# w1 and the transposed projections of a two-layer block: three 256-column products per weight tile instead of one of 512 and one of 256

## The chip, the core and the metric

The kernel runs on one core of one Trainium2 chip. The metric is the device time of one execution in microseconds (us); less is better. Three runs of the kernel before took 2183.35, 2184.06 and 2186.3 us, with a median of 2184.06 us.

## What is computed

A block of two layers on 256 tokens of width 2048 in fp32. Layer one is a stick-breaking attention with 16 heads, layer two a sparse attention with compressed, selected and windowed keys; behind each stands an MLP with a hidden width of 8192. Cut to what matters here:

```python
def sqrelu_mlp(h, w1, w2):
    return jnp.square(jax.nn.relu(h @ w1)) @ w2

q, k, v = jnp.split(h @ w_qkv, 3, axis=-1)                                # first attention
q, kc, vc, ks, vs, kw, vw, gl = jnp.split(h @ w_in, offs, axis=-1)        # second attention
...
h = h + attention(rms_norm(h, g))
h = h + sqrelu_mlp(rms_norm(h, mlp_norm_g[layer]), mlp_w1[layer], mlp_w2[layer])
```

The change touches `h @ w1` in both layers, q and k of three of the four head groups of the first attention, and kc and vc of the second.

## The kernel before, in words

Nearly all of the work is products of activations with weights that are read once from memory. To keep fp32 accuracy, each operand is split in two parts of type fp32r: hi, the rounded value, and lo, the rest. A product of x and w is the sum of three: hi by hi, hi by lo and lo by hi (the product of the two lo parts is left out).

Weights come in chunks of 128x1024 values (512 KB), either 2 row blocks of 512 columns (KC = 2, NB = 512) or 4 row blocks of 256 columns. SyncE issues the load (`load`, line 139) into a ring of five buffers; ScalarE copies hi into one of four buffers (line 134), VectorE subtracts lo into one of four (line 136). The two rings have 64 spare values (`PAD`) per buffer, so that a chunk can start at an offset: `NEAR` = 0, `FAR` = 16, `LOW` = 52, `SUM` = 48 values.

The activations of the first factor lie in `xs` as [128, 16 row blocks, 2, 256 tokens]: for each block of 128 rows the 256 columns of xhi and right behind them the 256 of xlo.

Where the result is wanted transposed (features on the partitions, tokens on the columns), a weight tile of 128x128 is the stationary operand and x moves:

- `proj_T2` (line 195), used by `group1` for w1: for two chunks at a time, 16 products of a hi tile with the 512 columns of xhi and xlo together (line 203), then 16 of a lo tile with the 256 columns of xhi (line 210). Each of the four 128-feature parts of a block has a PSUM bank of its own: the left half takes hi by xhi and lo by xhi, the right half hi by xlo.
- `proj_T2h` (line 216), used for q and k of head groups 1 to 3 and for kc and vc: the same on chunks of 4 row blocks by 256 columns (lines 224 and 230), with two banks.
- `chunk_T` (line 178), used for q and k of head group 0 alone, in the first stage, whose order of instructions is written out by hand: for each tile hi by xhi and hi by xlo, 256 columns each, then for all tiles lo by xhi (line 185). All three go into the same half bank; two features' parts share a bank. Its hi and lo lie at `FAR`.

As `proj_T2` leaves two halves to be added, `group1` copies the right half to SBUF on ScalarE (line 449) and adds it to the left on VectorE (line 450), four times for a block of 512 features; then one VectorE pass over 128x1024 takes the maximum with zero and multiplies with the token's norm factor (line 451). Squares, their split (lines 455 to 457) and sums for the Strassen form of a part of w2 (lines 462 to 465) follow. `evac_T2` (line 237) does the same for the projections: two copies (line 241), two additions (line 242) and a product with a row (line 243).

An MLP has four groups of 2048 hidden features; a group is `group1` (four blocks of 512 features, their banks taken in turn from the pools `acc` and `att`, four banks each) and then `group2`, the products with w2 (`chunk_N`, line 152, and `chunk_S`, line 245, with 256-column products at line 280). Work of other stages is put between the products by `pump` (line 106), which the product loops call after every eight or so products. Outside the first stage the compiler's scheduler sets each engine's order.

Of the kernel before, what the change touches and what calls it, by code (L numbers as in the profile page):

```python
# [25 lines left out]
KC = 2  # L26
# [13 lines left out]
def hybrid_kernel(  # L40
# [65 lines left out]
    def pump():  # L106
        if beside:
            b = beside[0]
            b[2] += b[1] / KC
            while b[2] >= 1:  # L110
                b[2] -= 1
                y = next(b[0], b)
                if y is b:
                    beside.remove(b)
                if y:
                    break
# [6 lines left out]

    PAD = 64
    NEAR, FAR, LOW, SUM = 0, 16, 52, 48

    def split(raw, o=(NEAR, NEAR)):  # L130
        n = KC * NB
# [14 lines left out]
    def load_split(*where, o=(NEAR, NEAR)):  # L146
        return split(load(*where), o)

    def bank(pool, tag):
        return pool.tile([P, NB], F32, tag=tag, name=tag)  # L150
# [24 lines left out]
                mm(ahi, lo[:, kk, :], k, t, False, last and kk == KC - 1)  # L175
            pump()

    def chunk_T(ps, src, k0, n0, first, last):

        hi, lo = src if isinstance(src, tuple) else load_split(src, k0, KC, n0, NB, o=(FAR, FAR))  # L180
        tiles = [(kk, m) for kk in range(KC) for m in range(NB // P)]

        def mm(w, x, kk, m, s, e):
            o = ps[m // 2][:, (m % 2) * T:(m % 2 + 1) * T]
            nc.tensor.matmul(o, w[:, kk, m * P:(m + 1) * P], x[:, k0 + kk, :], start=s, stop=e, skip_group_check=True)  # L185

        for kk, m in tiles:
            mm(hi, xhi, kk, m, first and kk == 0 and m % 2 == 0, False)
            mm(hi, xlo, kk, m, False, False)
        pump()  # L190
        for kk, m in tiles:
            mm(lo, xhi, kk, m, False, last and kk == KC - 1)
        pump()

    def proj_T2(ps, src, n0):


        for k0 in range(0, KD, 2 * KC):
            parts = [load_split(src, k0 + i * KC, KC, n0, NB, o=(NEAR, LOW)) for i in range(2)]
            tiles = [(k0 + i * KC + kk, m, *(a[:, kk, m * P:(m + 1) * P] for a in parts[i]))  # L200
                     for i in range(2) for kk in range(KC) for m in range(NB // P)]
            for j, (k, m, hi, lo) in enumerate(tiles):
                nc.tensor.matmul(  # L203
                    ps[m], hi, xs[:, k, :, :].rearrange("p a t -> p (a t)"), start=k == 0, stop=k == KD - 1,
                    skip_group_check=True,
                )
                if j % 8 == 7:
                    pump()
            for j, (k, m, hi, lo) in enumerate(tiles):
                nc.tensor.matmul(  # L210
                    ps[m][:, :T], lo, xhi[:, k, :], start=False, stop=k == KD - 1, skip_group_check=True,
                )
                if j % 8 == 7:
                    pump()

    def proj_T2h(src, n0):

        ps = [bank(acc, "acc") for _ in range(2)]
        KH, W = 2 * KC, NB // 2
        for k0 in range(0, KD, KH):  # L220
            hi, lo = load_split(src, k0, KH, n0, W, o=(NEAR, LOW))
            tiles = [(kk, m) for kk in range(KH) for m in range(2)]
            for kk, m in tiles:
                nc.tensor.matmul(  # L224
                    ps[m], hi[:, kk, m * P:(m + 1) * P], xs[:, k0 + kk, :, :].rearrange("p a t -> p (a t)"),
                    start=k0 + kk == 0, stop=k0 + kk == KD - 1, skip_group_check=True,
                )
            pump()
            for kk, m in tiles:
                nc.tensor.matmul(  # L230
                    ps[m][:, :T], lo[:, kk, m * P:(m + 1) * P], xhi[:, k0 + kk, :],
                    start=False, stop=k0 + kk == KD - 1, skip_group_check=True,
                )
            pump()
        return ps

    def evac_T2(dst, ps, row):

        c = small.tile([P, 2, T], F32, tag="part", name="part", bufs=1)
        for j in range(2):  # L240
            nc.scalar.activation(c[:, j, :], ps[j][:, T:], AF.Copy)
            nc.vector.tensor_tensor(dst[:, j, :], ps[j][:, :T], c[:, j, :], op=OP.add)
        nc.vector.tensor_tensor(dst, dst, row.unsqueeze(1).to_broadcast([P, 2, T]), op=OP.mult)

    def chunk_S(ps, src, k0, n0, first, last, ahi, alo, shi, slo, koff=0):

# [67 lines left out]
    def proj_N(src, n0, pool=acc, tag="acc"):  # L314
        ps = [bank(pool, tag) for _ in range(NT)]
        for k0 in range(0, KD, KC):
            chunk_N(ps, src, k0, n0, k0 == 0, k0 + KC == KD, xhi, xlo)
        return ps

    def proj_T(src, n0):  # L320
        ps = [bank(acc, "acc") for _ in range(2)]
        for k0 in range(0, KD, KC):
            chunk_T(ps, src, k0, n0, k0 == 0, k0 + KC == KD)
        return ps

    def split_evac(hi, lo, src, scale=None):
# [103 lines left out]
    def mlp(l, layer, junk, done, last=None):  # L430
# [9 lines left out]
        def group1(fg, pools):  # L440

            for fb in range(D // NB):
                ps = [bank(*pools[fb % 2]) for _ in range(NB // P)]
                proj_T2(ps, w1, fg * D + fb * NB)
                k, n = fb * (NB // P), NB // P
                a = junk.tile([P, n, T], F32, tag="pre", name="pre", bufs=1)
                for j in range(n):
                    c = junk.tile([P, T], F32, tag="part", name="part")
                    nc.scalar.activation(c, ps[j][:, T:], AF.Copy)
                    nc.vector.tensor_tensor(a[:, j, :], ps[j][:, :T], c, op=OP.add)  # L450
                nc.vector.scalar_tensor_tensor(
                    a, a, 0.0, row.unsqueeze(1).to_broadcast([P, n, T]), op0=OP.max, op1=OP.mult
                )
                s = junk.tile([P, n, T], F32, tag="sq", name="sq", bufs=1)
                nc.scalar.activation(s, a, AF.Square)
                nc.scalar.activation(yhi[:, k:k + n, :], s, AF.Copy)
                nc.vector.tensor_tensor(ylo[:, k:k + n, :], s, yhi[:, k:k + n, :].bitcast(F32), op=OP.subtract)

                sv = s.rearrange("p (j kk) t -> p j kk t", kk=2)
                a1, a2 = [[sv[:, :, kk, t * P:(t + 1) * P] for kk in (1, 0)] for t in range(NT)]  # L460
                q = junk.tile([P, 2, 4, P], F32, tag="sums", name="sums", bufs=1)
                nc.vector.scalar_tensor_tensor(q[:, :, 0, :], a2[0], -1.0, a2[1], op0=OP.mult, op1=OP.subtract)
                nc.vector.tensor_tensor(q[:, :, 2, :], a1[0], a2[0], op=OP.subtract)
                nc.vector.tensor_tensor(q[:, :, 1, :], a2[1], q[:, :, 2, :], op=OP.subtract)
                nc.vector.tensor_tensor(q[:, :, 3, :], a1[1], q[:, :, 1, :], op=OP.subtract)
                split_evac(ss[:, 0, k // 2:k // 2 + 2], ss[:, 1, k // 2:k // 2 + 2], q)
# [44 lines left out]
    with tc.tile_pool(name="sbp", bufs=2) as sp:  # L511
# [171 lines left out]
        for hg in range(NH // HG):  # L683
            qT = sp.tile([P, HG, T], F32, name="qT")
            kT = sp.tile([P, HG, T], F32, name="kT")
            v = sp.tile([P, NT, NB], F32, name="v")
            if hg == 0:
                spawn(first_factors(qT, kT), 1)
            else:
                for b in range(2):  # L690
                    evac_T2(qT[:, 2 * b:2 * b + 2, :], proj_T2h(sb_w_qkv[0], hg * NB + b * T), rows[:, 0, :])
                for b in range(2):
                    evac_T2(kT[:, 2 * b:2 * b + 2, :], proj_T2h(sb_w_qkv[0], D + hg * NB + b * T), rows[:, 1, :])
            psv = proj_N(sb_w_qkv[0], 2 * D + hg * NB, *((att, "att") if hg == 0 else ()))
            for t in range(NT):
                nc.scalar.activation(v[:, t, :], psv[t], AF.Copy, scale=factor[0][:, t:t + 1])

            drain()
            spawn(attention(hg, qT, kT, v), 0.6 if hg < NH // HG - 1 else 1.1)
# [20 lines left out]
    with tc.tile_pool(name="nsa", bufs=2) as ap, ExitStack() as last:  # L720
# [255 lines left out]
        for i in range(2):  # L976
            cT = cp.tile([P, G, T], F32, tag="cT", name="cT", bufs=1)
            for b in range(2):
                ps = proj_T2h(w_in, C0 + i * NB + b * T)
                if rstd is None:  # L980
                    rstd = make_rstd("nsa")
                    pb = bcast_rows(rstd)
                    rb = cp.tile([P, T], F32, name="rb2", bufs=1)
                    nc.scalar.activation(rb, pb[:, :T], AF.Copy)
                evac_T2(cT[:, 2 * b:2 * b + 2, :], ps, rb)
            spawn(compress(i, cT), 1.8)


# [117 lines left out]
```

## Time and profile before

| | us |
|---|---|
| median of three runs | 2184.06 |
| the profiled execution | 2184.25 |
| its span, first to last instruction | 2182.2 |
| TensorE products (PE) busy | 2172.6 |
| TensorE weight loads (PEld) busy | 1880.7 |
| VectorE (DVE) busy | 1524.8 |
| ScalarE (ACT) busy | 1210.8 |
| moved by DMA | 405.97 MB, mean 186 GB/s |

Products are pipelined: the time shown for one reaches to the end of its drain, beside which the next one already runs. What a product costs in a dense stretch is the time from its start to the next one's. Lines of the timeline merge products of one kind in succession: the first number is the start of the first, the second the time to the end of the last.

### The profile page before, as it was taken

The numbers are of one execution on the slowest core, as the hardware profiler recorded it, in microseconds if no ns is written. First come the engines' busy times: TensorE is split into PE (matmuls) and PEld (weight loads), VectorE is DVE, ScalarE is ACT, GpSimd is POOL, SyncE is SP. The second block draws the span as 40 slices with busy tenths as digits, with TensorE's granted clock in tenths as the row PEclk, the third lists the DMA queues.
The fourth block names the chain that finished last, engine by engine and source line by source line (L and its number), as shares of the span: only waits on it lengthen the run. The fifth ranks groups of instructions, "written<-read, shape, count | busy, mean of one in ns | idle before, by whom it ended". The sixth has DMA issues, their size and how long they took to land.

```text
span 2182.2 us, 31326 instructions
## 1 busy us (share of the span) xinstructions
PE 2172.6 (100%) x11922; PEld 1880.7 (86%) x11922; DVE 1524.8 (70%) x2096; ACT 1210.8 (55%) x1697; POOL 42.5 (2%) x75
## 2 busy tenths in 40 slices
PE   9999999999999999999999999999999999999999
PEld 9888888888888888888888888888888888888888
DVE  5656656677677677668777877755777676777685
ACT  5555665555455465456555666655554554654553
POOL 0000000000000000000000011000000000000000
PEclk9999999999999999999999999999999999999999
DMA  7655555565665665665667554456656656656664
GB/s 232 206 172 174 157 182 176 181 186 191 205 191 181 216 190 180 217 192 185 206 181 219 160 145 140 137 165 184 188 181 212 193 174 213 193 180 210 191 198 157
DMA packets 260766, 405.97 MB, mean 186 GB/s; under 512 B 13188, under 2 KB 91912, under 8 KB 260616
## 3 DMA queue, kind: packets, MB, share of 16 engines
q1 hardware_dynamic: 259800, 403.52, 59.6%
q8 instruction: 93, 1.52, 0.3%
q10 hardware_dynamic: 816, 0.46, 0.1%
q14 instruction: 57, 0.47, 0.1%
HBM read 401.83 MB, written 2.10 MB: 185 GB/s over the span
## 4 chain that ended last, share of the span: by engine, by line
PE 99%; DVE 0%; POOL 0%; ACT 0%; issue 0%; DVEq 0%; ACTq 0%; POOLq 0%
PE acc L156 31%; PE att L156 13%; PE acc L203 11%; PE att L203 11%; PE acc L210 5%; PE att L210 5%; PE acc L224 5%; PE att L280 4%; PE acc L280 4%; PE acc L230 3%; PE acc L185 2%; PE att L938 1%; PE att L343 1%; PE att L930 0%; PE att L931 0%; PE att L932 0%
## 5 line engine op out<-in xcount | busy, mean ns | idle before, releaser
L136 DVE TENSOR_TENSOR lo<-raw,hi 128x1024 fp32r<-128x1024 f32 x687 | 830.9, 1220 | 386.4 <-issue 170.0
L134 ACT ACTIVATE hi<-raw 128x1024 fp32r<-128x1024 f32 x687 | 726.5, 1059 | 655.7 <-PE acc L156 182.8
L156 PE MATMUL acc<-hi,yhi 128*128 128x512 f32 x640 | 250.7, 392 | 0.0
L156 PE MATMUL acc<-hi,ylo 128*128 128x512 f32 x640 | 249.2, 390 | 0.0
L203 PE MATMUL acc<-xs,hi 128*128 128x512 f32 x1024 | 243.8, 390 | 0.0
L203 PE MATMUL att<-xs,hi 128*128 128x512 f32 x1024 | 243.2, 390 | 0.0
L203 PEld LDWEIGHTS acc<-xs,hi 128*128 128x128 f32 x1024 | 187.8, 188 | 36.2 <-DVE h L399 0.3
L203 PEld LDWEIGHTS att<-xs,hi 128*128 128x128 f32 x1024 | 188.0, 188 | 35.9
L156 PE MATMUL acc<-hi,xs 128*128 128x512 f32 x704 | 177.1, 392 | 0.0
L156 PE MATMUL acc<-lo,yhi 128*128 128x512 f32 x640 | 172.4, 390 | 0.0
L156 PEld LDWEIGHTS acc<-hi,xs 128*128 128x128 f32 x704 | 130.3, 188 | 26.5
L156 PE MATMUL att<-hi,yhi 128*128 128x512 f32 x380 | 148.2, 390 | 0.0
L156 PE MATMUL att<-hi,ylo 128*128 128x512 f32 x380 | 147.9, 389 | 0.0
L156 PEld LDWEIGHTS acc<-lo,yhi 128*128 128x128 f32 x640 | 119.5, 188 | 24.9 <-issue 0.4
L134 ACT ACTIVATE hi<-ts 128x1024 fp32r<-128x1024 f32 x64 | 67.8, 1059 | 130.9 <-DVE ts L260 92.8
L156 PEld LDWEIGHTS acc<-hi,yhi 128*128 128x128 f32 x640 | 120.2, 188 | 23.3 <-ACT yhi L329 0.2
L156 PEld LDWEIGHTS acc<-hi,ylo 128*128 128x128 f32 x640 | 120.2, 188 | 23.2 <-DVE ylo L330 0.2
L210 PEld LDWEIGHTS att<-xs,lo 128*128 128x128 f32 x1024 | 128.4, 188 | 5.2
L254 DVE TENSOR_TENSOR ts<-raw 128x512 f32<-128x512 f32 x64 | 44.2, 691 | 126.3 <-DMA raw<-in_mlp_w_dram 126.3
L210 PEld LDWEIGHTS acc<-xs,lo 128*128 128x128 f32 x1024 | 128.2, 188 | 4.8
L210 PE MATMUL acc<-xs,lo 128*128 128x256 f32 x1024 | 130.1, 278 | 0.0
L210 PE MATMUL att<-xs,lo 128*128 128x256 f32 x1024 | 129.7, 278 | 0.0
(305 smaller groups left out, 3058.1 us busy)
## 6 DMA issues: line engine op xcount, KB each, us to landing
raw<-in_mlp_w_dram SPq DMA_DIRECT2D x512, 512.0 KB, 4.2
raw<-in_sb_w_qkv_dram SPq DMA_DIRECT2D x95, 512.0 KB, 4.0
raw<-in_nsa_w_in_dram SPq DMA_DIRECT2D x50, 512.0 KB, 3.6
raw<-in_sb_w_out_dram SPq DMA_DIRECT2D x32, 512.0 KB, 3.8
raw<-in_nsa_w_in_dram SPq DMA_DIRECT2D x64, 256.0 KB, 3.3
raw<-in_nsa_w_out_dram SPq DMA_DIRECT2D x32, 512.0 KB, 3.8
w1t<-in_nsa_cmp_w_dram SPq DMA_DIRECT2D x8, 512.0 KB, 4.8
h<-in_x_dram SPq DMA_DIRECT2D x8, 256.0 KB, 4.2
```

Of the source, the lines that this page charges most:

```text
L134: nc.scalar.activation(hi, raw, AF.Copy)
L136: nc.vector.tensor_tensor(lo, raw, hi.bitcast(F32), op=OP.subtract)
L156: mm = lambda a, b, k, t, s, e: nc.tensor.matmul(ps[t], a[:, k, t * P:(t + 1) * P], b, start=s, stop=e)
L185: nc.tensor.matmul(o, w[:, kk, m * P:(m + 1) * P], x[:, k0 + kk, :], start=s, stop=e, skip_group_check=True)
L203: nc.tensor.matmul(ps[m], hi, xs[:, k, :, :].rearrange("p a t -> p (a t)"), start=k == 0, stop=k == KD - 1, skip_group_check=True,)
L210: nc.tensor.matmul(ps[m][:, :T], lo, xhi[:, k, :], start=False, stop=k == KD - 1, skip_group_check=True,)
L224: nc.tensor.matmul(ps[m], hi[:, kk, m * P:(m + 1) * P], xs[:, k0 + kk, :, :].rearrange("p a t -> p (a t)"), start=k0 + kk == 0, stop=k0 + ...
L230: nc.tensor.matmul(ps[m][:, :T], lo[:, kk, m * P:(m + 1) * P], xhi[:, k0 + kk, :], start=False, stop=k0 + kk == KD - 1, skip_group_check=True,
L254: nc.vector.tensor_tensor(ts[:, :2, :], flat[:, W:3 * W].rearrange("p (a n) -> p a n", a=2), b12, op=OP.subtract)
L280: nc.tensor.matmul(ps[i], a, w, start=s, stop=e, skip_group_check=True)
L343: nc.tensor.transpose(ps[:, j * T + t * P:j * T + (t + 1) * P], h[:, t, (kp + j) * P:(kp + j + 1) * P], ident)
L938: nc.tensor.transpose(ptp[:w, j * P:(j + 1) * P], src(j), ident)
```

## The change

All transposed projections go through `chunk_T`, which now takes the number of row blocks of a chunk. `proj_T2`, `proj_T2h` and `evac_T2` go. The three products of a tile go into the same half bank, so a block of w1 holds two banks instead of four, and a halved projection one instead of two. The two halves are no longer copied and added; the VectorE passes read the sums from PSUM, for w1 in two passes of 128x512. The lo weights of these projections lie at `FAR` instead of `LOW`, the hi weights at `FAR` instead of `NEAR`. The scratch tiles "part" go. The diff, cut to its core:

```diff
-    NEAR, FAR, LOW, SUM = 0, 16, 52, 48
+    NEAR, FAR, SUM = 0, 16, 48
...
-    def chunk_T(ps, src, k0, n0, first, last):
+    def chunk_T(ps, src, k0, n0, first, last, nk=KC, o=None):
-        hi, lo = src if isinstance(src, tuple) else load_split(src, k0, KC, n0, NB, o=(FAR, FAR))
-        tiles = [(kk, m) for kk in range(KC) for m in range(NB // P)]
+        nm = KC * NB // P // nk
+        hi, lo = src if isinstance(src, tuple) else load_split(src, k0, nk, n0, nm * P, o=o or (FAR, FAR))
+        tiles = [(kk, m) for kk in range(nk) for m in range(nm)]
...
+    def proj_T(ps, src, n0, nk=KC, o=None):
+        for k0 in range(0, KD, nk):
+            chunk_T(ps, src, k0, n0, k0 == 0, k0 + nk == KD, nk, o)
+
+    def proj_Th(src, n0):
+        ps = bank(acc, "acc")
+        proj_T([ps], src, n0, 2 * KC)
         return ps
 
+    def evac_T(dst, ps, row):
+        nc.vector.tensor_tensor(
+            dst, ps.rearrange("p (m t) -> p m t", m=2), row.unsqueeze(1).to_broadcast([P, 2, T]), op=OP.mult
+        )
...
         def group1(fg, pools):
-                ps = [bank(*pools[fb % 2]) for _ in range(NB // P)]
-                proj_T2(ps, w1, fg * D + fb * NB)
+                ps = [bank(*pools[fb % 2]) for _ in range(NB // P // 2)]
+                proj_T(ps, w1, fg * D + fb * NB)
-                for j in range(n):
-                    c = junk.tile([P, T], F32, tag="part", name="part")
-                    nc.scalar.activation(c, ps[j][:, T:], AF.Copy)
-                    nc.vector.tensor_tensor(a[:, j, :], ps[j][:, :T], c, op=OP.add)
-                nc.vector.scalar_tensor_tensor(
-                    a, a, 0.0, row.unsqueeze(1).to_broadcast([P, n, T]), op0=OP.max, op1=OP.mult
-                )
+                for j in range(0, n, 2):
+                    nc.vector.scalar_tensor_tensor(
+                        a[:, j:j + 2, :], ps[j // 2].rearrange("p (m t) -> p m t", m=2), 0.0,
+                        row.unsqueeze(1).to_broadcast([P, 2, T]), op0=OP.max, op1=OP.mult,
+                    )
...
-                    evac_T2(qT[:, 2 * b:2 * b + 2, :], proj_T2h(sb_w_qkv[0], hg * NB + b * T), rows[:, 0, :])
+                    evac_T(qT[:, 2 * b:2 * b + 2, :], proj_Th(sb_w_qkv[0], hg * NB + b * T), rows[:, 0, :])
```

kT of the first attention and cT of the second change as qT does.

## Rows read from the trace of the kernel before

**Rows 1.** The page: busy shares, granted clock in 40 slices, chain by engine.
```profile
PE 2172.6 (100%) x11922; PEld 1880.7 (86%) x11922; DVE 1524.8 (70%) x2096; ACT 1210.8 (55%) x1697; POOL 42.5 (2%) x75
...
PEclk9999999999999999999999999999999999999999
...
PE 99%; DVE 0%; POOL 0%; ACT 0%; issue 0%; DVEq 0%; ACTq 0%; POOLq 0%
```

**Rows 2.** Waits of PE, whole span: us in total, times, longest.
```profile
PE acc L185 <- ACT hi L134: 1.9, 1, 1.9
PE att L531 <- POOL ident masks.py:199: 1.6, 1, 1.6
PE att L803 <- DVE hs L799: 0.9, 1, 0.9
PE att L838 <- DVE kc L834: 0.5, 1, 0.5
PE acc L280 <- DVE slo L261: 0.4, 1, 0.4
PE acc L550 <- ACT hi L543: 0.2, 1, 0.2
```

**Rows 3.** Groups by line: the 512-column products (count, busy us, mean ns).
```profile
L203 PE MATMUL acc<-xs,hi 128*128 128x512 f32 x1024 | 243.8, 390 | 0.0
L203 PE MATMUL att<-xs,hi 128*128 128x512 f32 x1024 | 243.2, 390 | 0.0
...
L224 PE MATMUL acc<-xs,hi 128*128 128x512 f32 x512 | 128.2, 392 | 0.0
```

**Rows 4.** Stretches: length, busy us (instructions touched) by engine, clock, DMA share, GB/s.
```profile
50.10:56.46 6.36, 6.36 (x59) 6.36 (x58) 5.50 (x8) 6.26 (x14) 0.71 (x1) 1.00 0.60 186
419.05:485.13 66.08, 66.08 (x387) 58.44 (x385) 47.27 (x59) 38.19 (x46) 0.00 (x0) 1.00 0.62 191
1109.33:1136.93 27.60, 27.60 (x162) 24.36 (x161) 20.82 (x32) 12.93 (x19) 0.00 (x0) 1.00 0.69 190
```

**Rows 5.** Timeline of PE, two chunks of w1.
```profile
441.07 3.80 PE L203 MATMUL acc<-xs,hi 128*128 128x512 f32 x16
444.71 2.03 PE L210 MATMUL acc<-xs,lo 128*128 128x256 f32 x16
446.58 3.80 PE L203 MATMUL acc<-xs,hi 128*128 128x512 f32 x16
```

**Rows 6.** Timeline of PE, first stage, head group 0.
```profile
52.83 1.07 PE L185 MATMUL acc<-xs,lo 128*128 128x256 f32 x8
53.73 1.98 PE L185 MATMUL acc<-xs,hi 128*128 128x256 f32 x16
55.55 1.07 PE L185 MATMUL acc<-xs,lo 128*128 128x256 f32 x8
```

**Rows 7.** Timeline of PE, 256-column products of w2 and of the compression.
```profile
510.08 0.87 PE L280 MATMUL att<-hi,ss 128*128 128x256 f32 x6
510.79 0.28 PE L280 MATMUL att<-hi,yhi 128*128 128x256 f32 x1
...
1137.86 0.64 PE L792 MATMUL att<-ws,bs 128*120 128x256 f32 x4
1138.33 0.86 PE L1001 MATMUL acc<-xs,gw 128*96 128x512 f32 x3
```

**Rows 8.** Groups by line: work behind the products, and a like pass from PSUM.
```profile
L449 ACT ACTIVATE part<-acc 128x256 f32<-128x256 f32 x64 | 22.0, 383 | 13.1 <-DVE pre L450 7.3 <-PE acc L210 5.8
...
L450 DVE TENSOR_TENSOR pre<-acc,part 128x256 f32<-128x256 f32 x64 | 23.9, 415 | 0.0
...
L451 DVE SCALAR_TENSOR_TENSOR pre<-pre,row 128x1024 f32<-128x1024 f32 x32 | 39.1, 1223 | 0.8
...
L642 DVE SCALAR_TENSOR_TENSOR s<-att,e 128x512 f32<-128x512 f32 x8 | 5.5, 691 | 20.6 <-ACT e L637 20.6
```

**Rows 9.** Timeline of DVE, lo splits in w1.
```profile
434.89 2.36 DVE L136 TENSOR_TENSOR lo<-raw,hi 128x1024 fp32r<-128x1024 f32 x2 [2.01 <-issue]
```

More of the change, by code (lines that the diff above doesn't have):

```diff
@@ L191, in chunk_T @@
         for kk, m in tiles:
-            mm(lo, xhi, kk, m, False, last and kk == KC - 1)
+            mm(lo, xhi, kk, m, False, last and kk == nk - 1)
         pump()
[L195 to L205, printed above, removed]
-                )
[L207 to L234, printed above, removed]
-        return ps
@@ L237, in evac_T2 @@
[L237 to L243, printed above, removed]
+    def proj_T(ps, src, n0, nk=KC, o=None):
+        for k0 in range(0, KD, nk):
+            chunk_T(ps, src, k0, n0, k0 == 0, k0 + nk == KD, nk, o)
@@ L317, in proj_N @@
             chunk_N(ps, src, k0, n0, k0 == 0, k0 + KC == KD, xhi, xlo)
[L318 to L323, printed above, removed]
         return ps
@@ L442, in group1 @@
             for fb in range(D // NB):
-                ps = [bank(*pools[fb % 2]) for _ in range(NB // P)]
-                proj_T2(ps, w1, fg * D + fb * NB)
+                ps = [bank(*pools[fb % 2]) for _ in range(NB // P // 2)]
+                proj_T(ps, w1, fg * D + fb * NB)
                 k, n = fb * (NB // P), NB // P
                 a = junk.tile([P, n, T], F32, tag="pre", name="pre", bufs=1)
-                for j in range(n):
-                    c = junk.tile([P, T], F32, tag="part", name="part")
-                    nc.scalar.activation(c, ps[j][:, T:], AF.Copy)
-                    nc.vector.tensor_tensor(a[:, j, :], ps[j][:, :T], c, op=OP.add)
-                nc.vector.scalar_tensor_tensor(
-                    a, a, 0.0, row.unsqueeze(1).to_broadcast([P, n, T]), op0=OP.max, op1=OP.mult
-                )
+                for j in range(0, n, 2):
[3 more added lines that the diff above has]
+                    )
                 s = junk.tile([P, n, T], F32, tag="sq", name="sq", bufs=1)
@@ L690, in hybrid_kernel @@
                 for b in range(2):
-                    evac_T2(qT[:, 2 * b:2 * b + 2, :], proj_T2h(sb_w_qkv[0], hg * NB + b * T), rows[:, 0, :])
+                    evac_T(qT[:, 2 * b:2 * b + 2, :], proj_Th(sb_w_qkv[0], hg * NB + b * T), rows[:, 0, :])
                 for b in range(2):
-                    evac_T2(kT[:, 2 * b:2 * b + 2, :], proj_T2h(sb_w_qkv[0], D + hg * NB + b * T), rows[:, 1, :])
+                    evac_T(kT[:, 2 * b:2 * b + 2, :], proj_Th(sb_w_qkv[0], D + hg * NB + b * T), rows[:, 1, :])
             psv = proj_N(sb_w_qkv[0], 2 * D + hg * NB, *((att, "att") if hg == 0 else ()))
@@ L978, in hybrid_kernel @@
             for b in range(2):
-                ps = proj_T2h(w_in, C0 + i * NB + b * T)
+                ps = proj_Th(w_in, C0 + i * NB + b * T)
                 if rstd is None:
@@ L984, in hybrid_kernel @@
                     nc.scalar.activation(rb, pb[:, :T], AF.Copy)
-                evac_T2(cT[:, 2 * b:2 * b + 2, :], ps, rb)
+                evac_T(cT[:, 2 * b:2 * b + 2, :], ps, rb)
             spawn(compress(i, cT), 1.8)
```

## The prediction

> **What bounds the kernel now.** I read the page's busy shares, its clock line and its chain first, then the list of what TensorE waited for, then the pace of TensorE in the stages that the change touches. TensorE is busy for the whole span, no slice is below the highest tenth, the granted clock is at its upper level (2.4 GHz) throughout, and 99% of the chain is PE [rows 1]. The waits of PE add up to 5.5 us in six places [rows 2]; none is at lines 203, 210, 224 or 230, which the change replaces. So time is the sum of what TensorE's products cost from start to start. The busy times and means of the groups won't do for that: a 512-column product shows about 390 ns because its drain lies beside the next product. I take start-to-start times from stretches that hold one kind of work alone.
>
> In such a stretch of w1 (three blocks of 512 columns, 12 pairs of chunks, 192 weight tiles of 128x128) a tile costs 66.08/192 = 344.2 ns; in one of the halved projections (10 chunks, 80 tiles) 27.60/80 = 345.0 ns [rows 4]. The timeline splits a pair of chunks: sixteen 512-column products take 444.71 - 441.07 = 3.64 us, 227.5 ns each, and sixteen 256-column products 446.58 - 444.71 = 1.87 us, 116.9 ns each [rows 5].
>
> The kernel already holds the new form. The first q and k projections run chunk_T (line 185): every tile in three products of 256 columns, hi by xhi, hi by xlo, lo by xhi, all into one sum. The stretch from 50.10 to 56.46 us is 8 + 24 + 24 = 56 of these and nothing else: 6.36/56 = 113.6 ns each [rows 4]. It is the same in both kinds of run: 16 products with hi in 1.82 us and 8 with lo in 0.90 us [rows 6]. A new tile at this price is 3 x 113.6 = 340.7 ns.
>
> **The change, part by part.**
>
> *The products.* There are 1024 + 1024 tiles of w1 and 512 of the halved projections, one for each 512-column product [rows 3]. Each gives up one product of 512 and one of 256 columns and gets three of 256. By the rows above w1 gains 2048 x (344.2 - 340.7) = 7.1 us and the projections 512 x (345.0 - 340.7) = 2.2 us: together 9.3 us, all on the path, since PE is the path. Where it comes from: two products of 256 (227.2) cost what one of 512 did (227.5), so the split of the wide product is free, and the gain is the lo product, 116.9 down to 113.6.
>
> What I choose here is the price of a 256-column product, because the trace has two. Line 185 gives 113.6 ns. Line 210 gives 116.9, and the Strassen chunks (line 280: six in 510.79 - 510.08 = 0.71 us) and the compression (line 792: four in 1138.33 - 1137.86 = 0.47 us) give 118 [rows 5, 7]. I take line 185. It is the very function that the change calls, with the same chunk of 2 x 512, the same offset FAR for hi and lo in the same ring of four buffers, the same xs as moving operand, and the same splits on ACT and DVE and a like transfer rate beside it (186 GB/s against 191) [rows 4]. Line 210 differs in just what the change alters: its lo weights lie at offset LOW, and its results go to four banks in turn. The ends for the range: 113.3 (24 in 1.82 + 0.90 us) makes 11.2 us of gain, 113.75 (16 in 1.82 us) makes 7.9; the far end, 116.9 for all, is a rival below.
>
> The trace shows no fixed cost for a product beside its columns where the two forms meet: 227.5 ns for 512, 113.6 for 256 [rows 4, 5]. The Trainium skill ("TensorE: Matmul & The Clock Gate", section Back-to-back issue gap) says otherwise: columns over 2.4 GHz and 2.5 ns more for each product, so cutting one in two adds 2.5 ns. By that the sum would be 2560 x 2.5 = 6.4 us slower; the row of this chip's run decides, and it does not agree.
>
> *The halved projections* use chunks of 4 x 256. Their tiles lie one after the other in the buffer as in a chunk of 2 x 512, but the sums of a tile alternate between two halves of one bank instead of four halves of two. No row shows that; the run with hi writes the same half twice in succession at line 185 already, at full pace, so I take no cost. The bound is the 2.2 us of this part, and 512 x 3 x 3.3 ns (116.9 against 113.6) = 5.1 us if all of it ran at line 210's pace.
>
> *The weight loads.* One more for each tile, 2560 in all. At line 185 each of its products has a load of its own too, so the 113.6 ns holds it.
>
> *What follows the products.* For each of 32 blocks of w1, four ACT copies (383 ns) and four DVE additions (415) go, and one DVE pass over 128x1024 (1223) becomes two over 128x512 from PSUM (nearest row 691) [rows 8]: DVE 2.88 us down to 1.38, ACT 1.53 down to 0. I cost it at nothing: PE waited for none of it [rows 2]. The 16 blocks of the halved projections lose two copies, two additions and a pass for one pass. Cover gone, it would be the 1.4 us a block. The saving too is off the path, so "no addition of two parts" buys nothing by itself.
>
> *Splits, queues and buffers.* SP issues the same loads, 512 KB each, ACT and DVE make the same splits; only their rate rises, by 1%. The lo of a chunk is needed 1.82 us into it [rows 6], where before it was needed after two chunks' hi products, 3.64 us. The new DVE passes wait for a block's last product, and splits may queue behind them. The lead is larger: the two lo splits of 434.89 us are for the run of 444.71 us [rows 5, 9], 7 us after they end. Half as many banks are held per block, so nothing new waits there. Two scratch tiles go, which moves later buffers by 2 KB; at line 185 the pace is one over weight tiles 512 bytes apart, so I expect nothing.
>
> Sum: the profiled execution took 2184.25 us (span 2182.2), less 9.3 is 2174.95; the median of the runs is 0.2 us lower, so **2174.8 us**.
>
> **The rivals.** About 0.2%, 4.4 us, is what a measurement of this kernel can tell from no change: 2179.7 and 2188.4 are the bounds.
>
> *Only hi gets line 185's pace.* If lo products cost 116.9 for a reason that stays (what lies around w1, not the weights' offset or the banks), a tile is 227.2 + 116.9 = 344.1, and only the projections gain: 2048 x 0.1 + 512 x 0.9 = 0.7 us, 2183.4. For it: every lo product outside the first stage is at that pace. Against: in the first stage lo runs at 113 with the same splits beside it. 0.08.
>
> *Each product has a fixed cost, and line 210 is the true price.* From 512 c + f = 227.5 and 256 c + f = 116.9 comes f = 6.3 ns. This is the mechanism of the skill's page above, at a larger size. It decides wherever a 512-column product is cut in two: a tile would be 3 x 116.9 = 350.7, w1 13.3 us and the projections 2.9 us slower, **2200.3 us**. For it: lines 210, 280 and 792 agree, three places with other operands [rows 5, 7]. Against: line 185, which alone has the new form. It would need something that makes the first stage special, such as its hand-written order. 0.10.
>
> *The split comes late at a block's end.* If DVE had no lead, a block's passes (2 x 0.69) and the next lo split (1.22) would end some 2.6 us and the drain after its last product, 1 us later than lo is due: 32 us over 32 blocks of w1, some 2207 in all. It decides from a lead under 1 us; the trace has 7. 0.03.
>
> **How the numbers follow.** The forecast has 0.79 (own range 2172 to 2178.5: the two ends of the pace, 2172.9 and 2176.2, and 1 to 2 us for a reordered queue), the rivals 0.08, 0.10 and 0.03. The range runs from 2172 to 2184: that holds the forecast and the rival of no change and leaves out the slower ones. Faster 0.79, same 0.08, slower 0.13.
>
> **What would show it.** In the profile after: 24 products of line 185 from start to start in 2.73 us within w1, 5.46 for two chunks instead of 5.51; no waits of PE at the blocks' ends; ACT about 60 us less busy (128 copies of 383 ns and 32 at the projections). A pace of 116 to 117 ns at line 185 in w1 makes the prediction wrong, as would PE waiting for lo at a block's end.

## The result and the profile after

The changed kernel takes 2195.94 us in the median of four runs (2193.65 to 2198.36), beside 2183.78 us of the kernel before on the same chip. The ratio is 1.0053 with a 95% interval of 1.0036 to 1.0071: it is slower by half a per cent, and the time lies outside the predicted range, on the other side of no change.

The page of the changed kernel, busy shares and chain by engine:

```profile
PE 2186.2 (100%) x14482; PEld 1997.6 (91%) x14482; DVE 1484.1 (68%) x1968; ACT 1164.7 (53%) x1537; POOL 42.5 (2%) x75
...
PE 99%; DVE 0%; POOL 0%; ACT 0%; issue 0%; DVEq 0%; ACTq 0%; POOLq 0%
```

Set beside [rows 1], nothing changed in kind: PE is busy throughout and is the chain, with 2560 more products. Its longest waits are the first of [rows 2] again. So the 12 us are not a stall. They must be in the pace of the products, and there the changed kernel shows something that [rows 4] did not. Three stretches of w1: the part of the first group of MLP one behind the last transposes, a later group of MLP one, and one of MLP two. Columns are length, busy us by engine, clock, DMA share and GB/s.

```profile
413.63:486.51 72.88, 72.88 (x646) 72.88 (x644) 48.15 (x54) 37.77 (x38) 0.00 (x0) 1.00 0.67 194
571.60:662.05 90.45, 90.45 (x769) 90.45 (x768) 57.12 (x62) 43.57 (x43) 0.00 (x0) 1.00 0.65 190
1839.87:1930.33 90.46, 90.46 (x770) 90.46 (x769) 56.36 (x61) 43.59 (x43) 0.00 (x0) 1.00 0.65 190
```

The first stretch is 643 products in 72.88 us: 113.3 ns each, the low end of the forecast. The other two are whole groups of 768 products in 90.45 us: 117.8 ns each. Code, shapes, clock and offsets are the same, and the work beside them nearly so. Six of the eight groups run at the slow pace from end to end; the first group of each MLP starts at it too and is at the fast one from the first transposes among its products on. At the pace of before a group takes four blocks of 66.08/3 us [rows 4], 88.1 us. So each late group loses 2.4 us, 14.2 us in six of them, while the first groups and the halved projections gain 3.3 us. The profiled span is 12.9 us longer. What is left lies elsewhere: the first stage ended 3.2 us later than before, and the w2 stages of MLP two took about 1 us less. The start differs from execution to execution (the first stage ended between 56.2 and 59.6 us in the profiles of the changed kernel and its variants). Here the granted clock was 0.62 in the mean over the second chunk of line 185, below the upper level (1.00) of the stretches above, and the chunk took 4.45 us where it took 2.85 before.

The timeline of PE in the changed kernel shows both paces, first the start of a late group, then the start of a halved projection, which begins slow and turns fast:

```profile
571.60 2.05 PE L185 MATMUL att<-xs,hi 128*128 128x256 f32 x16
573.48 1.11 PE L185 MATMUL att<-xs,lo 128*128 128x256 f32 x8
574.43 2.05 PE L185 MATMUL att<-xs,hi 128*128 128x256 f32 x16
...
1101.07 2.05 PE L185 MATMUL acc<-xs,hi 128*128 128x256 f32 x16
1102.95 1.11 PE L185 MATMUL acc<-xs,lo 128*128 128x256 f32 x8
...
1105.78 0.60 PE L303 MATMUL att<-ident,h 128*128 128x128 f32 x4
...
1107.14 0.60 PE L303 MATMUL att<-ident,h 128*128 128x128 f32 x4
1107.50 2.07 PE L185 MATMUL acc<-xs,hi 128*128 128x256 f32 x16
1109.41 1.07 PE L185 MATMUL acc<-xs,lo 128*128 128x256 f32 x8
1110.32 1.86 PE L185 MATMUL acc<-xs,hi 128*128 128x256 f32 x15
```

Read the starts, as ever. At 571.60 sixteen products take 1.88 us and eight take 0.95. At 1109.41 eight take 0.91, and the pace stays there. What stands between is transposes of other work (line 303), put in by `pump`: four at 1105.78, after which the products settle at 113 to 114 ns from start to start, and four more at 1107.14. Before the slow stretches shown stand 512-column products of w2. That gave theory M: a run of 256-column products has two paces, keeps the one it starts with, and the start is decided by what goes ahead.

### The profile page after: what moved, and what is told of

It is laid out like the page before. It is cut to its first block, busy times and chain, and to the rows that moved or that the text cites. A ratio compares the mean times of both kernels' runs of the same rounds, so it can differ in the third digit from the quotient of the medians.

```text
span 2195.1 us, 36040 instructions
## 1 busy us (share of the span) xinstructions
PE 2186.2 (100%) x14482; PEld 1997.6 (91%) x14482; DVE 1484.1 (68%) x1968; ACT 1164.7 (53%) x1537; POOL 42.5 (2%) x75
## 4 chain that ended last, share of the span: by engine, by line
PE 99%; DVE 0%; POOL 0%; ACT 0%; issue 0%; DVEq 0%; ACTq 0%; POOLq 0%
PE acc L155 31%; PE acc L185 26%; PE att L185 16%; PE att L155 13%; PE acc L246 4%; PE att L246 4%; PE att L896 1%; PE att L303 1%; PE att L888 0%; PE att L889 0%; PE att L890 0%; PE att L583 0%; PE att L631 0%; PE att L842 0%; PE att L844 0%; PE att L843 0%
## 5 line engine op out<-in xcount | busy, mean ns | idle before, releaser
L185 PE MATMUL acc<-xs,hi 128*128 128x256 f32 x3312 | 420.4, 280 | 1.9 <-ACT hi L133 1.9
L185 PEld LDWEIGHTS acc<-xs,hi 128*128 128x128 f32 x3312 | 400.1, 189 | 2.7 <-ACT hi L133 2.1
L185 PE MATMUL att<-xs,hi 128*128 128x256 f32 x2048 | 259.8, 280 | 0.0
L185 PEld LDWEIGHTS att<-xs,hi 128*128 128x128 f32 x2048 | 248.3, 189 | 0.3
L185 PE MATMUL acc<-xs,lo 128*128 128x256 f32 x1656 | 226.5, 279 | 0.0
L185 PEld LDWEIGHTS acc<-xs,lo 128*128 128x128 f32 x1656 | 207.4, 189 | 0.0
L185 PE MATMUL att<-xs,lo 128*128 128x256 f32 x1024 | 140.4, 280 | 0.0
```

## The experiments

**Four transposes ahead of each group.**

```diff
+                if fb == 0:
+                    for _ in range(4):
+                        nc.tensor.transpose(ps[0][:, :P], ident, ident)
                 proj_T(ps, w1, fg * D + fb * NB)
```

> Edit: the changed kernel, with four 128-column transposes of the identity ahead of each of the eight groups of w1, into the bank that the first product then overwrites. Theory M: a run of 256-column products keeps the pace it starts with, 113.4 ns after a transpose, 117.8 ns after a 512-column product. Then the six late groups of w1 fall from 90.45 us to about 87.1 us and 0.45 us for the transposes, and the time from 2195.9 to about 2179 us. Rival O: the pace is set by something steady in those groups (where operands lie, what runs beside them). Then they stay at 90.45 us and the transposes are added: about 2199 us.

Measured: 2178.94 us (five runs), 0.9965 of the kernel before (0.9952 to 0.9979). Two late groups from their first product to their last, and the start of the first of them:

```profile
570.36:657.50 87.14, 87.14 (x772) 87.14 (x769) 55.92 (x61) 43.36 (x42) 0.00 (x0) 1.00 0.68 195
2000.17:2087.31 87.14, 87.14 (x772) 87.14 (x769) 56.80 (x63) 43.23 (x42) 0.00 (x0) 1.00 0.66 190
```
```profile
570.00 0.60 PE L406 MATMUL att<-ident 128*128 128x128 f32 x4
570.36 2.08 PE L185 MATMUL att<-xs,hi 128*128 128x256 f32 x16
572.27 1.07 PE L185 MATMUL att<-xs,lo 128*128 128x256 f32 x8
573.18 1.98 PE L185 MATMUL att<-xs,hi 128*128 128x256 f32 x16
```

All six late groups fell from 90.45 to 87.14 us, for 0.36 us of transposes. Nothing else in the groups was touched, so what runs beside them, their banks and their buffers are not by themselves what made them slow. Theory M gave both the pace and the time; rival O, as stated, falls.

**The offsets of before.** `o=o or (FAR, FAR)` becomes `o=o or (NEAR, LOW)` in the changed kernel.

> Edit: the changed kernel, with the weights of all transposed projections at the offsets of before (hi at NEAR, lo at LOW, instead of both at FAR). Theory M: nothing moves; first groups of w1 at 113.4 ns a product, late ones at 117.8, about 2196 us. Rival O, in the form of the prediction (the offset makes the lo product 116.9 ns): lo products of the first groups go to about 117 ns, 16 of 24 products stay at 113.4, and the first groups get about 0.9 us longer each.

Measured: 2213.89 us, 1.0125 of the kernel before (1.0112 to 1.0139). Both were wrong about this: M said that nothing moves, O that only lo does. Lo went to 117.4 ns, which is O's figure, but hi went to 119.2. A late group:

```profile
576.88:667.98 91.10, 91.10 (x769) 91.09 (x768) 56.74 (x61) 43.61 (x43) 0.00 (x0) 1.00 0.65 189
```

That is 118.6 ns a product in the mean, and the first groups, with the same transposes among their products, are there too (behind their last transposes 648 products take 76.9 us, 118.7 ns each). At these offsets the transposes find no fast pace to switch to. Theory M needs a second half (M2): the offset decides whether the fast pace exists, the start whether a run gets it.

**Other things ahead.** A helper issues, into the bank that is overwritten next, transposes or fp32r products of hi x by x:

```diff
+            if fb == 2 and fg == 0:
+                mm(1, xhi, NB)
+                if l == 1:
+                    tr(4)
+            if fb == 0 and fg > 0:
+                if l == 0:
+                    (None, lambda: tr(1), lambda: tr(2), lambda: mm(1, xhi, P))[fg]()
+                else:
+                    (None, lambda: mm(4, xhi, P), lambda: mm(1, xhi, P // 2), lambda: mm(4, xhi, NB))[fg]()
```

> Edit: the changed kernel, with another thing ahead of each late group of w1. MLP one: group 1 one transpose, group 2 two transposes, group 3 one fp32r product of 128 columns. MLP two: group 1 four fp32r products of 128 columns, group 2 one of 64 columns, group 3 four of 512 columns. In group 0 of both, one 512-column product ahead of block 2, in MLP two followed by four transposes. Theory M: MLP one, group 0 runs at 113.4 ns in blocks 0 and 1 and at 117.8 from the 512-column product on; MLP two, group 0 stays at 113.4; group 3 of MLP two stays at 117.8. Open is which of the others do it: if any product shorter than a weight load does, all five are at 113.4; if only transposes do, groups 1 and 2 of MLP one. Rival O: all late groups at 117.8, both groups 0 at 113.4 throughout.

Measured (one run, 2196.41 us): group 1 of MLP one, with one transpose, was fast, the five others slow. The three late groups of MLP one (one transpose, two, one product of 128 columns):

```profile
570.29:657.42 87.13, 87.13 (x770) 87.13 (x769) 56.32 (x61) 43.66 (x43) 0.00 (x0) 1.00 0.68 197
742.66:833.20 90.54, 90.54 (x772) 90.54 (x771) 56.08 (x61) 43.41 (x43) 0.00 (x0) 1.00 0.65 189
918.35:1008.86 90.51, 90.51 (x771) 90.51 (x770) 57.16 (x63) 43.57 (x43) 0.00 (x0) 1.00 0.65 187
```

And the two insertions inside the first groups, MLP one and MLP two:

```profile
441.39 0.40 PE L405 MATMUL acc<-xs 128*128 128x512 f32 x1
441.63 1.99 PE L185 MATMUL acc<-xs,hi 128*128 128x256 f32 x16
443.45 1.07 PE L185 MATMUL acc<-xs,lo 128*128 128x256 f32 x8
...
1531.44 0.40 PE L405 MATMUL acc<-xs 128*128 128x512 f32 x1
1531.67 0.60 PE L401 MATMUL acc<-ident 128*128 128x128 f32 x4
1532.02 2.13 PE L185 MATMUL acc<-xs,hi 128*128 128x256 f32 x16
1533.99 1.11 PE L185 MATMUL acc<-xs,lo 128*128 128x256 f32 x8
1534.93 2.05 PE L185 MATMUL acc<-xs,hi 128*128 128x256 f32 x16
```

M's two statements about the first groups were both wrong, and in opposite ways. One 512-column product did not end the fast pace (0.91 us for eight lo products behind it), and the same product followed by four transposes did (0.94 us, to the end of the group). So it is not a kind of instruction that sets the pace, such as 512 columns slow, transpose fast. Some finer condition of the first few products does, and what goes ahead shifts it. The trace of the changed kernel says the same, in each of its three halved head groups: behind two 512-column and four 256-column products of the attention (lines 612 to 619) a run is at 113.5 ns from its start (103.28, 176.15 and 249.03 us); four 256-column and four 128-column products of lines 583 and 584 bring the fast pace behind the slow one (119.56 us), and the like of lines 631 and 632 the slow pace behind the fast one (114.48 us).

**The number of transposes.** Three, five and six ahead of groups 1 to 3 of MLP one, and one, two and seven in MLP two (`for _ in range(n)` around the transposes of the first experiment).

> Edit: the changed kernel, with n transposes ahead of each late group of w1: 3, 5 and 6 in MLP one, 1, 2 and 7 in MLP two. Theory M2 (a run has two paces, its start decides by its timing, and it keeps the pace): each late group runs at 113.4 or at 117.8 ns from its third product to its end, nothing between; 1 gives 113.4 and 2 gives 117.8 in MLP two as they did in MLP one, 3, 5, 6 and 7 are open. Rival K (a transpose ahead is what counts, and two of them were an accident): all six groups at 113.4. Rival R (chance): 1 and 2 need not repeat.

Measured: 2181.85 us in one run. The three late groups of MLP two (one, two, seven):

```profile
1655.04:1742.17 87.13, 87.13 (x770) 87.13 (x769) 56.62 (x61) 43.66 (x43) 0.00 (x0) 1.00 0.67 197
1827.41:1917.94 90.53, 90.53 (x771) 90.53 (x770) 56.60 (x61) 43.48 (x43) 0.00 (x0) 1.00 0.65 189
2003.73:2090.87 87.14, 87.14 (x772) 87.14 (x769) 56.49 (x62) 43.34 (x42) 0.00 (x0) 1.00 0.67 192
```

MLP one's three were fast. One and two repeated what they did in MLP one, which speaks against chance. But each count had stood in the same group number both times, so count and place were still confounded.

**One transpose ahead of every late group.**

> Edit: the changed kernel, with one transpose ahead of each of the six late groups of w1. Theory M2: all six at 113.3 ns, 87.1 us with 0.2 us for the transpose; against four transposes about 0.3 us less in each of six groups and 0.4 us less in the first groups: about 2176 to 2178 us, 0.3 to 0.4% under the kernel before. If the start were chance, some groups would be at 90.5 us and the time 3.4 us longer for each.

Measured: 2184.39 us (11 runs), 0.9994 of the kernel before (0.9985 to 1.0003); the expectation was 7 us too low. Groups 1 and 3 were fast in both MLPs, group 2 slow in both. In MLP one group 3 took 87.15 us, and group 2:

```profile
742.64:833.18 90.54, 90.54 (x771) 90.54 (x769) 56.00 (x61) 43.26 (x43) 0.00 (x0) 1.00 0.65 190
```

So one transpose is enough in some places and not in others.

**Two or three.** Two, three and two in MLP one, two, three and three in MLP two.

> Edit: the changed kernel, with two, three and two transposes ahead of groups 1 to 3 of MLP one and two, three and three ahead of those of MLP two. Group 2 stayed slow with one and with two, groups 1 and 3 were fast with one. Reading C (three or more always start fast, one or two depend on what stands around them): group 2 fast with three in both; groups 1 and 3 open with two. Reading G (group 2 alone is hard to start; groups 1 and 3 start fast with any number): all six at 113.3 ns, and the time about 1 us under the version with four transposes, 0.35 to 0.4% under the kernel before. If two is a bad number wherever it stands, groups 1 and 3 of MLP one and group 1 of MLP two stay at 90.5 us, some 10 us more.

Measured: 2179.66 us (eight runs), 0.9971 (0.9960 to 0.9981). MLP one:

```profile
571.75:658.88 87.13, 87.13 (x771) 87.13 (x769) 55.54 (x61) 43.01 (x43) 0.00 (x0) 1.00 0.67 197
744.22:831.37 87.15, 87.15 (x771) 87.15 (x770) 55.32 (x60) 42.79 (x43) 0.00 (x0) 1.00 0.67 196
916.61:1007.14 90.53, 90.53 (x771) 90.53 (x770) 57.13 (x63) 43.48 (x43) 0.00 (x0) 1.00 0.66 187
```

Reading C holds and G falls: group 3 is slow with two, group 1 fast with two, and wherever three or more stood ahead of a group at offset 16 it was fast. That holds for the starts of groups behind w2; inside a group the four transposes of the third experiment, behind a single 512-column product, ended the fast pace.

**Three ahead of every late group.** `range(3 if fb == 0 and fg else 0)`.

> Edit: the changed kernel, with three transposes ahead of each of the six late groups of w1. If three always start a run fast (four did in six groups out of six, three in four out of four), all six are at 113.3 ns and the time is 3.4 us under the version with two or three, one of whose groups stayed slow: about 2176 to 2177 us beside 2186 of the kernel before, a ratio of 0.995 to 0.997. Each group that starts slow adds 3.4 us.

Measured: 2176.89 us (five runs), 0.9957 of the kernel before (0.9944 to 0.9971); all six late groups fast. The first of MLP one and the last of MLP two:

```profile
568.44:655.57 87.13, 87.13 (x771) 87.13 (x770) 56.27 (x61) 43.43 (x43) 0.00 (x0) 1.00 0.67 196
1997.46:2084.61 87.15, 87.15 (x772) 87.15 (x770) 56.92 (x63) 43.32 (x43) 0.00 (x0) 1.00 0.66 191
```

This version beats both kernels, and it lands 2 us above the time that the prediction gave the change itself.

**Offsets with nothing ahead.** Late groups of the changed kernel with hi and lo at 8, 32 and 48 values in MLP one, 24, 40 and 56 in MLP two (the parameter `o` of `proj_T`).

> Edit: the changed kernel, with hi and lo of the late groups of w1 at other offsets, nothing ahead of them: 8, 32 and 48 values in MLP one, 24, 40 and 56 in MLP two. Theory M2: after the 512-column products of w2 at least the offsets near 16 start slow, 117.8 ns; if an offset has no slow pace, its group runs at 113.4 ns (87.1 us) without any help. Rival O (the offset alone sets the pace): paces differ by offset and none is 113.4, since 16 was chosen and gives 117.8 there.

Measured: 2199.54 us in one run. Offsets 32, 48 and 56:

```profile
744.36:836.53 92.17, 92.17 (x769) 92.17 (x768) 56.12 (x61) 43.34 (x43) 0.00 (x0) 1.00 0.65 186
921.64:1012.09 90.45, 90.45 (x770) 90.45 (x769) 57.27 (x63) 43.56 (x43) 0.00 (x0) 1.00 0.65 186
...
2016.96:2106.55 89.59, 89.59 (x769) 89.59 (x768) 57.21 (x63) 43.48 (x43) 0.00 (x0) 1.00 0.65 188
```

Divided by 768 these are 120.0, 117.8 and 116.7 ns; the others lay at 117.3 to 120.0. No offset tried is fast without help. Offset 48 takes the very time of 16.

**Offsets with four transposes ahead.** (0, 0), (16, 52) and (0, 16) for hi and lo in MLP one, (32, 32), (48, 48) and (8, 8) in MLP two.

> Edit: the changed kernel, with four transposes ahead of each late group of w1, and hi and lo at (0, 0), (16, 52) and (0, 16) in MLP one, (32, 32), (48, 48) and (8, 8) in MLP two. Theory M2: a run of products can be at 113.4 ns only where its weights lie at an offset that has the fast pace: with (0, 0) all at about 118.6; with (16, 52) hi at 113.4 and lo at about 117; with (0, 16) hi at 118.6 and lo at 113.4 or slow. Rival: the four transposes alone decide, then all six groups run at 113.4.

Measured: 2196.89 us in one run. The groups with (0, 0), (16, 52) and (48, 48):

```profile
570.50:662.73 92.23, 92.23 (x772) 92.23 (x770) 56.92 (x63) 43.20 (x42) 0.00 (x0) 1.00 0.64 185
748.18:836.18 88.00, 88.00 (x772) 88.00 (x770) 55.44 (x61) 42.75 (x42) 0.00 (x0) 1.00 0.66 194
...
1842.14:1929.27 87.13, 87.13 (x772) 87.13 (x770) 55.96 (x61) 43.25 (x42) 0.00 (x0) 1.00 0.67 196
```

The timeline of the one with (16, 52):

```profile
751.03 1.98 PE L185 MATMUL acc<-xs,hi 128*128 128x256 f32 x16
752.85 1.09 PE L185 MATMUL acc<-xs,lo 128*128 128x256 f32 x8
753.78 1.98 PE L185 MATMUL acc<-xs,hi 128*128 128x256 f32 x16
```

Hi at 16 takes 1.82/16 = 113.8 ns, lo at 52 takes 0.93/8 = 116.3, side by side in one group: each run of products goes by its own weights' offset. (48, 48) is fast, (0, 0), (0, 16), (32, 32) and (8, 8) are not, at 91 to 92.2 us a group. In (0, 16) lo, behind hi at 0, is at the slow 117.9 ns. Offset 32 too took two times, 92.17 us without transposes and 91.23 with four (in another group), neither of them fast. The rival, that the transposes alone decide, falls; M2 holds but for sizes ((0, 0) is at 120.0, not 118.6).

**The kernel before, transposes ahead of lo runs.** Four transposes between the hi and the lo run in the four pairs of chunks of one block.

> Edit: the kernel before, with four transposes ahead of the four runs of lo products of one block of w1 (MLP one, group 1, block 2). Theory M: these four runs go from 116.9 ns to about 113.4 ns a product from the second or third product on, with everything else about the products as it was, the offset LOW and the four banks too; the time stays within 3 us of 2184. Rival O: they stay at 116.9 ns.

Measured: 2185.94 us in one run; one of the four:

```profile
617.32 0.60 PE L211 MATMUL acc<-ident 128*128 128x128 f32 x4
617.67 2.12 PE L213 MATMUL att<-xs,lo 128*128 128x256 f32 x16
619.63 3.84 PE L203 MATMUL att<-xs,hi 128*128 128x512 f32 x16
```

Sixteen lo products take 1.96 us, with the 0.09 us that a first one behind transposes costs: 1.87, as in [rows 5]. M as first stated was wrong here, for the reason that the offsets showed: at 52 no fast pace was seen, with transposes ahead or without.

**The kernel before, lo at 16.** `LOW` = 16 in place of 52, nothing else.

> Edit: the kernel before, with its lo weights at offset 16 (the place of the changed kernel) instead of 52; nothing else. The prediction's reading (offset 52 is what makes line 210 slow): lo products go from 116.9 to about 113.5 ns, 8 us less. Theory M2: each lo run starts right behind 512-column products, as the late groups of the changed kernel do, so it starts slow, at 117.8: 2 us more, which is at the edge of what the measurement tells.

Measured: 2189.54 us (ten runs), 1.0017 (1.0008 to 1.0027): slower by about 4 us.

```profile
592.91 3.82 PE L203 MATMUL acc<-xs,hi 128*128 128x512 f32 x16
596.56 2.05 PE L210 MATMUL acc<-xs,lo 128*128 128x256 f32 x16
598.45 3.82 PE L203 MATMUL acc<-xs,hi 128*128 128x512 f32 x16
```

Lo takes 1.89 us, 118 ns each, where it took 1.87 at offset 52, and the wide products 3.65 where they took 3.64. Behind wide products, at least as this kernel places them, a lo run starts slow, and there 52 is the better place. The prediction's reading of line 210, that the place alone makes it slow, falls. Transposes ahead of lo at 16 were not tried in this kernel.

**The copies and additions put back.** On the version with one transpose, four copies and four additions behind each block of w1, results unused.

> Edit: the changed kernel with one transpose, and the four copies and four additions of each block of w1 put back behind its products (their results are not used), scratch tiles too. Theory: they lie beside the products and no product waits for them; within 2 us of the same kernel without them. Rival (the additions were worth something): 1 us or more for each of 32 blocks.

Measured: 2186.52 us (ten runs, 2183.70 to 2189.92) beside 2184.39 (2182.91 to 2187.55). A median 2 us higher is at the edge of what was expected, and the spreads overlap. The groups of w1 took the same times as without them; the profiled execution had one wait of 2.5 us of PE in a w2 chunk, where DVE was late behind a load. So the additions cost nothing at the blocks themselves, far from 1 us each; whether they delay a chunk of w2 now and then stays open.

## Why the prediction was wrong

- **What bounds the kernel** was right: PE, with no wait at the changed lines, before and after.
- **The price of a 256-column product** is the step that failed: "I take line 185", 113.6 ns. This was measured correctly, and it is the price in the first groups and in most of the projections. It is not the price of the function: the same code in six groups takes 117.8. The three reasons given (same function, same offset, same work beside it) were true of those groups too and did not fix the pace. What differs is how a run starts. Every run of line 185 in [rows 6] belongs to a stage with transposes of x between its chunks; a late group of w1 starts behind 512-column products and has no transposes. The trace of before held the warning. Its first chunk of line 185, which starts right behind 24 products of line 550 and no transposes, is at the slow pace, at a granted clock of 1.00:

```profile
10.19 2.05 PE L185 MATMUL acc<-xs,hi 128*128 128x256 f32 x16
12.07 1.11 PE L185 MATMUL acc<-xs,lo 128*128 128x256 f32 x8
13.02 0.60 PE L343 MATMUL att<-ident,h 128*128 128x128 f32 x4
```

  Here 24 products take 13.02 - 10.19 = 2.83 us, 117.9 ns each, on the very line and at the very offset. The prediction took its price from a stretch near the stage's end, called it one pace, and never asked whether all chunks of the line had it.
- **The reading of line 210** was wrong in its conclusion. Its lo weights are at a place where no fast pace was seen, but the new place was no better behind wide products: moving them alone cost time instead of saving 8 us. The gain per tile rested on this. Line 210 differs from line 185 in one more thing, which the prediction did not list: each of its runs follows sixteen 512-column products [rows 5].
- **The rival of a fixed cost per product** came nearest in time (2200.3) and in its price, 116.9 ns beside the 117.8 of the late groups. Its mechanism is not what the runs show: with three transposes ahead, two products of 256 columns cost 226.7 ns, no more than one of 512. What it said it would need, something that makes the first stage special, was there: the transposes. Nor did the Trainium skill's 2.5 ns for each product ("TensorE: Matmul & The Clock Gate", Back-to-back issue gap), given there for an isolated product and not for a stream with weight loads, show up in the fast groups.
- **The weight of the other rows.** Lines 280 and 792 [rows 7] showed 118 ns with other operands, three places against one. They were set aside because only line 185 had the new form. A price that several places contradict, seen in one stage alone, was given 0.79 where its condition was unknown.
- **The rest.** The halved projections gained 1.4 us instead of 2.2, since parts of each run slow. The late split cost nothing: no wait of PE at any block's end. ACT's busy time fell by 46 us against "about 60": the durations of its instructions together fell by 60, but they overlap, and busy time counts an overlap once.

The sum itself comes out once the start is mended. In the version with three transposes the eight groups of w1 are 7.6 us shorter than before, where 7.1 was forecast, the halved projections 1.4 us, where 2.2 was, and the transposes take 0.25 us ahead of each of six groups. Its time is 2176.89 us beside the forecast of 2174.8. That the two agree so closely is in part luck, since the start alone moves an execution by some 3 us.

## What to carry to other kernels

When one line shows two paces, find out what sets them before using either as a price: ask what goes ahead of each run, not only what runs beside it. In a PE-bound kernel of short products, look at the start-to-start time of a whole run in every stage after a change; a steady 4% can be a matter of how the run began, and a few cheap instructions ahead of it can turn it. Tune weight offsets and order together: an offset that is best behind wide products (52 here) need not be best in a uniform run (16 here, with transposes ahead).

## What the runs showed of the hardware

Not expected: a run of 256-column fp32r products with a weight load each has two steady paces, 113.3 and 117.8 ns, and held either through 768 products and some 90 us, over changes of bank, pool and buffer. At the start of a group one or two 128-column transposes gave the fast pace in some places and not in others, the same way each time they were tried; three or more gave it in every group at offset 16. Inside a group, behind one 512-column product, four of them ended it. The fast pace outlasted one 512-column product, and two with four of 256 columns. The fast pace was seen with weights at offsets 16 and 48 (32 values apart) and at none of 0, 8, 32 and 52; without transposes the other offsets tried lay between 116.7 and 120.0 ns.

The records of the weight loads show where the 4.5 ns sit. At the fast pace each product starts 110 ns after the start of its own load, and each load lasts 187 or 188 ns (all of some 740 in a group of the version with four transposes). At the slow pace a product starts 114 or 115 ns after its load, and every third load lasts 192 ns (a late group of the changed kernel). Which of the two is cause and which effect, these records do not say.

What in the chip decides is open. The runs show that it lies in what goes ahead of a run, settled within its first six or so products, and in the weights' place in the buffer; none of them separates how loads and products mesh from other causes, and offsets 24, 40 and 56 were not tried with transposes ahead.
